# Issuing a small DRAM round trip of an attention from GpSimd instead of SyncE

## The chip, the cores and the metric

The program runs on one core of a Trainium2 chip. The metric is device time of one execution in microseconds (us); lower is better. Before the change it is 3516.77 us, the median of 3 runs (3515.63 to 3521.61). The engines are TensorE (PE, matmuls), VectorE (DVE), ScalarE (ACT), GpSimd (POOL) and SyncE (SP, which here only issues DMAs). Each engine works through its own instruction queue in order; a DMA is issued from one of these queues and then runs by itself.

## What is computed

The reference runs two blocks over a sequence of 1024 tokens of width 1024. The first block (attention and mixture of experts) is not touched. The second has two layers; each normalises the input, projects it with `w_in`, feeds three mixers (retention, a latent-query attention `mla`, and a gated linear attention), multiplies their outputs with SiLU gates and projects with `w_out`. The change is in `mla`:

```python
def block(args):                                   # one block of 128 queries, 8 heads
    qn, qp, i0 = args
    sc = (jnp.einsum('bqhd,bkhd->bhqk', qn, k_nope)
          + jnp.einsum('bqhd,bkd->bhqk', qp, k_pe)).astype(jnp.float32) * scale
    q_chunk = (i0 + jnp.arange(Q_BLOCK)) // CHUNK
    mask = key_chunk[None, :] <= q_chunk[:, None]
    sc = jnp.where(mask, sc, -jnp.inf)
    p = jax.nn.softmax(sc, axis=-1).astype(v.dtype)
    return jnp.einsum('bhqk,bkhe->bqhe', p, v)
...
mixed = jnp.concatenate([r_o * jax.nn.silu(rz), m_o * jax.nn.silu(mz),
                         g_o * jax.nn.silu(gz)], axis=-1)
x = x + gate[:, None, :] * (mixed @ w_out[l])
```

## The kernel before

`mla` (from L1580) works on four pairs of heads, each with 16 tiles (2 heads by 8 blocks of 128 queries), in one loop over 68 steps at L1723. Step n does three things: `out(n-4)`, `scores(n)` and `turn(n-2)`. `scores` computes the 128 rows of scores on PE (L1751 to L1755), their maximum on DVE (L1757) and the exponent on ACT (L1759), which also leaves each row's sum in a column of `sm`; the tile `p` serves long rows, `ps` short ones. `turn` transposes the exponents on PE (L1783) and copies them out of PSUM with ACT, either at L1785 or as a high and a low part (L80 on ACT, L81 on DVE). `out` multiplies with the values (L1795 for short rows, L1804 for long ones; copies and adds at L1797, L1806, L1807) into `u0` and `u1`. The exponents are not normalised there: the division is done once per pair, on the output.

For that, at the last tile of a pair (n % 16 == 15), `attend_sums` (L1762) takes the 128x16 sums: DVE forms reciprocals (L1765), PE transposes them (L1767), ACT copies the result to `rt`, 16x128 (L1769), a DMA stores it to DRAM (`rrd`, L1770), and two DMAs load each head's 1024 numbers back, repeated over 64 partitions (L1773), into `rb`, a tile with the tag `lo`. Nothing else passes through `rrd`. Four steps later `out` loads the gate `z` (L1707), multiplies it by `rb` on POOL (L1708) and calls `store_mix` (L1303):

```python
(eng or nc.vector).tensor_tensor(z, v, z, op=ALU.mult)
hi, lo = self.t4("tb"), self.t4("lo")
g.split(z, hi.bitcast(F32R), lo.bitcast(F32R), eng)
nc.sync.dma_start(self.mixd[0, chunk * P:chunk * P + P], hi)
nc.sync.dma_start(self.mixd[1, chunk * P:chunk * P + P], lo)
```

`eng` is POOL for the first three pairs (L1306 on POOL, then ACT writes `tb` at L80, then POOL `lo` at L81) and DVE for the fourth. The stores (L1309, L1310) go to chunk 2 + pair of `mixd`.

The same loop prefetches `w_out` in 1 MB pieces from steps 42, 52 and 58 and after the loop (`load_out`, L1816, two loads of 512 KB on SP each; the last piece into tiles `p`), and `split_out` makes parts `r` from them (ACT, POOL or DVE). When the attention is over, `layer` (L1862) loads `mixd` (`load_mix`, L1834, tiles `mx`; the first chunks are 128x5x128 floats, 320 KB, once for each of the two parts) and multiplies with `w_out` (`products`, matmuls `acc<-r,mx` at L85 to L87). Chunk 5, which the fourth pair writes, is multiplied last for the first two row blocks and is loaded separately.

The program is written as if in one order; a scheduler then sets the order on each engine from its own estimates and adds the waits. So moving a DMA to another queue can also move instructions on engines that the edit does not name.

Of the kernel before, what the change touches and what calls it, by code (L numbers as in the profile page):

```python
# [19 lines left out]
S = 1024  # L20
D = 1024
P = 128
# [1149 lines left out]
class Second:  # L1172
# [589 lines left out]
    def attend_sums(self, pair, sums, pool):  # L1762

        g, nc = self.g, self.g.nc
        nc.vector.reciprocal(sums, sums)  # L1765
        tp = self.PSs.tile([P, 512], F32, tag="S", name=g.name("rt"))
        nc.tensor.transpose(tp[0:16, 0:P], sums.rearrange("p h t -> p (h t)"), g.ident)  # L1767
        r = pool.tile([16, P], F32, tag="rt", name=g.name("rt"))
        nc.scalar.activation(r, tp[0:16, 0:P], AF.Copy)  # L1769
        nc.sync.dma_start(self.rrd[pair].rearrange("h (t c) -> (h t) c", c=P), r)  # L1770
        rb = self.t4("lo")
        for q in range(2):
            nc.sync.dma_start(rb[64 * q:64 * q + 64], self.rrd[pair, q:q + 1].broadcast_to([64, S]))  # L1773
        return rb

    def attend_turn(self, p, i, pT):
# [345 lines left out]
```

## Time and profile before

| | |
|---|---|
| runs: median (lowest to highest) | 3516.77 us (3515.63 to 3521.61) |
| profiled execution: its own time | 3515.97 us |
| its span | 3514.2 us |
| PE busy | 3299.4 us (94%) |
| ACT busy / DVE busy / POOL busy | 1825.6 / 2407.2 / 829.2 us |
| mean granted PE clock | 0.967 of full speed |
| last attention matmul of `mla`, first layer | ends at 2737.17 us of the span |
| last attention matmul of `mla`, second layer | ends at 3402.75 us of the span |

The span is the time between the first and the last instruction that the profile shows; 1.8 us of the execution's own time lie outside it. PE is the busiest engine by far, so the question for any stage is what PE waits for there. In a timeline row, the bracket at the end gives how long the engine had been idle before that instruction and what ended the idle time; a name followed by q (SPq, POOLq) is the engine's issuing queue. A DMA's row shows only its issue: when its data landed is seen from who waited for it. "L1773" is a line of the kernel; `rrd<-rt` reads "into rrd, from rt".

### The profile page before, as it was taken

The page shows a single profiled execution, that of the slowest core. Times are in us where ns is not written, and L with a number is a line of the kernel's source. Part 1 is how long each engine was busy: PE and PEld are TensorE (multiplying, and loading weights), DVE is VectorE, ACT ScalarE, POOL GpSimd, SP SyncE. Part 2 cuts the span into 40 slices and gives each one's busy share as a digit, 9 for nine tenths or more (in the row PEclk, how much of TensorE's full clock was granted, in tenths as well). Part 3 has the DMA queues.
Part 4 walks back from the last instruction along what each step waited for, and adds up shares of the span by engine and source line. Part 5 has one row for each costly group of instructions (what it writes and reads, how often), then busy time and mean ns, then how long its engine had stood idle before and what let it go on. Part 6 is the DMA issues. An engine that isn't in the chain of part 4 may idle for free. (4 is left out here: it accounts for less than half of the span.)

```text
span 3514.2 us, 44298 instructions
## 1 busy us (share of the span) xinstructions
PE 3299.4 (94%) x16904; PEld 2730.2 (78%) x16904; DVE 2407.2 (69%) x2850; ACT 1825.6 (52%) x2601; POOL 829.2 (24%) x627
## 2 busy tenths in 40 slices
PE   8999999999999969999999993999999899998988
PEld 7888878888888857888888882877777788676776
DVE  5665888799999975679999996532366443425653
ACT  3224872588878733248778772122467212244751
POOL 1121221133333231113333326321002122400120
PEclk9999999999999989999999996999999999999999
DMA  8666524699999832179999984211322632023144
GB/s 260 216 188 173 146 87 162 248 389 381 380 379 378 303 128 77 75 265 381 388 387 382 376 314 170 37 31 38 116 73 91 203 91 43 19 81 108 61 138 156
DMA packets 302967, 695.86 MB, mean 198 GB/s; under 512 B 57518, under 2 KB 154576, under 8 KB 286300
## 3 DMA queue, kind: packets, MB, share of 16 engines
q1 hardware_dynamic: 263964, 634.11, 51.8%
q0 software_dynamic: 36480, 50.45, 4.3%
q10 hardware_dynamic: 2304, 8.39, 0.6%
q8 instruction: 136, 2.23, 0.3%
q14 instruction: 83, 0.68, 0.1%
HBM read 625.59 MB, written 98.66 MB: 206 GB/s over the span
## 5 line engine op out<-in xcount | busy, mean ns | idle before, releaser
L81 DVE TENSOR_TENSOR wcut<-wraw,wcut 128x2048 fp32r<-128x2048 f32 (+1 forms) x401 | 902.7, 2267 | 66.7 <-ACT wcut L80 66.7
L80 ACT ACTIVATE wcut<-wraw 128x2048 fp32r<-128x2048 f32 (+1 forms) x401 | 754.0, 1900 | 124.8 <-PE accy L87 98.1
L85 PE MATMUL gu<-wcut,xgh 128*128 128x512 f32 x1024 | 408.7, 399 | 0.4 <-ACT xgh L80 0.4
L87 PE MATMUL gu<-wcut,xgl 128*128 128x512 f32 x1024 | 403.8, 394 | 0.0
L86 PE MATMUL gu<-wcut,xgh 128*128 128x512 f32 x1024 | 401.3, 392 | 0.0
L806 POOL DMA_INDIRECT yd<-yo,idx x64 | 171.4, 2679 | 799.8 <-DVE yo L805 780.2
L85 PE MATMUL A<-h,whi 128*128 128x512 f32 (+1 forms) x736 | 287.3, 391 | 6.2 <-ACT h L80 3.3
L87 PE MATMUL A<-h,wlo 128*128 128x512 f32 (+1 forms) x736 | 281.8, 383 | 3.8 <-DVE wlo L81 3.8
L86 PE MATMUL A<-h,whi 128*128 128x512 f32 (+1 forms) x736 | 282.8, 384 | 0.9 <-DVE h L81 0.9
L80 ACT ACTIVATE whi<-wraw 128x1024 fp32r<-128x1024 f32 (+2 forms) x86 | 70.9, 856 | 310.7 <-PE A L86 251.4
L85 PEld LDWEIGHTS gu<-wcut,xgh 128*128 128x128 f32 x1024 | 193.9, 189 | 38.4 <-ACT xgh L80 0.8
L86 PEld LDWEIGHTS gu<-wcut,xgh 128*128 128x128 f32 x1024 | 192.8, 188 | 39.3
L87 PEld LDWEIGHTS gu<-wcut,xgl 128*128 128x128 f32 x1024 | 192.4, 188 | 39.7 <-DVE xgl L81 0.9
L81 DVE TENSOR_TENSOR wlo<-wraw,whi 128x1024 fp32r<-128x1024 f32 (+2 forms) x86 | 83.1, 973 | 200.8 <-ACT whi L80 200.5
L87 PE MATMUL accy<-wcut,hl 128*128 128x512 f32 x512 | 201.9, 394 | 0.3 <-DVE hl L81 0.3
L86 PE MATMUL accy<-wcut,hh 128*128 128x512 f32 x512 | 200.6, 392 | 0.0
L85 PE MATMUL accy<-wcut,hh 128*128 128x512 f32 x512 | 199.1, 389 | 1.6 <-ACT hh L80 1.6
L746 POOL DMA_INDIRECT xg<-hd,idx x64 | 182.7, 2854 | 49.3 <-DVE idx L736 30.4
L85 PEld LDWEIGHTS A<-h,whi 128*128 128x128 f32 x736 | 144.8, 197 | 34.6 <-ACT h L80 4.5
L87 PEld LDWEIGHTS A<-h,wlo 128*128 128x128 f32 x736 | 143.8, 195 | 31.5 <-DVE wlo L81 4.7
L86 PEld LDWEIGHTS A<-h,whi 128*128 128x128 f32 x736 | 144.5, 196 | 27.6 <-issue 3.1
L1708 POOL TENSOR_TENSOR z<-z,lo 128x1024 f32<-128x1024 f32 x8 | 19.0, 2375 | 471.4 <-DMA lo<-rrd 235.8
(518 smaller groups left out, 7835.9 us busy)
## 6 DMA issues: line engine op xcount, KB each, us to landing
wraw<-in_moe_w_gate SPq DMA_DIRECT2D x128, 1024.0 KB
wraw<-in_moe_w_up SPq DMA_DIRECT2D x128, 1024.0 KB
wraw<-in_moe_w_down SPq DMA_DIRECT2D x128, 1024.0 KB
spare<-in_ada_w SPq DMA_DIRECT2D x48, 512.0 KB
wraw<-in_w_in SPq DMA_DIRECT2D x40, 512.0 KB
y<-yd SPq DMA_DIRECT2D x16, 1024.0 KB
wraw<-in_attn_w_qkv SPq DMA_DIRECT2D x12, 1024.0 KB
mx<-mixd SPq DMA_DIRECT2D x24, 512.0 KB
```

Of the source, the lines that this page charges most:

```text
L80: self.nc.scalar.activation(hi, src, AF.Copy)
L81: (lo_eng or self.nc.vector).tensor_tensor(lo, src, hi.bitcast(F32), op=ALU.subtract)
L85: mm(out, wh, xh, start=start, stop=False)
L86: mm(out, wh, xl, start=False, stop=False)
L87: mm(out, wl, xh, start=False, stop=stop)
L746: self.g.nc.gpsimd.indirect_dma_start(out=xg, out_offset=None, in_=self.hd, in_offset=bass.IndirectOffsetOnAxis(ap=idx, axis=0), bounds_ch ...
L806: st = nc.gpsimd.indirect_dma_start(out=self.yd, out_offset=bass.IndirectOffsetOnAxis(ap=yidx, axis=0), in_=y, in_offset=None, bounds_chec ...
L1708: nc.gpsimd.tensor_tensor(z, z, rb, op=ALU.mult)
```

## The change

In `attend_sums`, the store of the reciprocals and both broadcast loads are issued from POOL's queue instead of SP's. It runs for four pairs in each of two layers: 8 stores of 8 KB and 16 loads of 256 KB.

```diff
--- before.py
+++ after.py
@@ -1767,10 +1767,10 @@
         nc.tensor.transpose(tp[0:16, 0:P], sums.rearrange("p h t -> p (h t)"), g.ident)
         r = pool.tile([16, P], F32, tag="rt", name=g.name("rt"))
         nc.scalar.activation(r, tp[0:16, 0:P], AF.Copy)
-        nc.sync.dma_start(self.rrd[pair].rearrange("h (t c) -> (h t) c", c=P), r)
+        nc.gpsimd.dma_start(self.rrd[pair].rearrange("h (t c) -> (h t) c", c=P), r)
         rb = self.t4("lo")
         for q in range(2):
-            nc.sync.dma_start(rb[64 * q:64 * q + 64], self.rrd[pair, q:q + 1].broadcast_to([64, S]))
+            nc.gpsimd.dma_start(rb[64 * q:64 * q + 64], self.rrd[pair, q:q + 1].broadcast_to([64, S]))
         return rb
 
     def attend_turn(self, p, i, pT):
```

The scheduler's order moves with it. SP's queue at the end of the attention (first layer, fourth pair; `p` is the last piece of w_out, `mx` the first loads of `mixd`):

```order
 L1816 DMA p_23042<-in_w_out 128x2x512
 L1816 DMA p_23043<-in_w_out 128x2x512
-L1770 DMA rrd<-rt_22967 16x128
-L1773 DMA lo_22970<-rrd 64x1024 x2
 L1834 DMA mx_23078<-mixd 128x5x128 x2
 L1834 DMA mx_23078<-mixd 128x2x128 x2
```

The store and the two loads of the sums are gone from between the last w_out loads and the first `mx` loads.

ACT's queue in the second pair of the first layer, where the first pair's `tb` (the high part of its gated output) is made:

```order
 L80 ACTIVATE r_21236<-T_21710 128x4x128
-L80 ACTIVATE r_21236<-T_21717 128x3x128
-L1759 ACTIVATE p_21708,sm_21576<-S_21698,mx_21706 128x768
 L80 ACTIVATE tb_21667<-z_21660 128x1024
 L1806 ACTIVATE u_3820_21685<-o_21687 128x128
+L1759 ACTIVATE p_21708,sm_21576<-S_21698,mx_21706 128x768
+L80 ACTIVATE r_21236<-T_21717 128x3x128
+L1797 ACTIVATE u_3821_21686<-o_21723 64x128
 L1759 ACTIVATE ps_21733,sm_21576<-S_21726,mx_21731 128x384
 L1785 ACTIVATE r_21075<-T_21735 128x256
 L1759 ACTIVATE p_21759,sm_21576<-S_21749,mx_21757 128x640
```

`tb` and the copy behind it moved ahead of the 128x768 exponent and the 128x3x128 copy; the first two pairs of both layers read alike. In the third pair `tb` keeps its place, and there a 128x512 copy (L1785) moved ahead of the split of a w_out load.

POOL's queue in the third and fourth pairs of the first layer:

```order
 L81 TENSOR_TENSOR r_22684<-wo_22680,r_22683 128x1024
+L1770 DMA rrd<-rt_22512 16x128
+L1773 DMA lo_22515<-rrd 64x1024 x2
 L1708 TENSOR_TENSOR z_22616<-z_22616,lo_22515 128x1024
 L1306 TENSOR_TENSOR z_22616<-u_3919_22158,z_22616 128x1024
 L81 TENSOR_TENSOR lo_22624<-z_22616,tb_22623 128x1024
+L1770 DMA rrd<-rt_22967 16x128
+L1773 DMA lo_22970<-rrd 64x1024 x2
```

The three DMAs stand directly before the multiplication that needs them, behind the splits of the earlier w_out loads; the other pairs read alike, without the splits.

## Rows read from the trace of the kernel before

**Rows 1.** The page's busy time, share of the span and instructions of each engine.
```profile
PE 3299.4 (94%) x16904; PEld 2730.2 (78%) x16904; DVE 2407.2 (69%) x2850; ACT 1825.6 (52%) x2601; POOL 829.2 (24%) x627
```

**Rows 2.** PE's waits, 2540 to 3514: us in total, times, longest us.
```profile
PE acc L85 <- DMA mx<-mixd: 16.5, 4, 5.4
...
PE S L1751 <- ACT ps L1759: 10.1, 8, 2.9
```

**Rows 3.** SP's timeline, first layer: start us, us, engine line op out<-in, count.
```profile
2609.08 0.30 SPq L1770 DMA_DIRECT2D rrd<-rt  x1
2610.44 1.12 SPq L1773 DMA_DIRECT2D lo<-rrd  x2
...
2696.29 0.42 SPq L1770 DMA_DIRECT2D rrd<-rt  x1
2700.06 1.09 SPq L1773 DMA_DIRECT2D lo<-rrd  x2
...
2729.43 3.71 SPq L1816 DMA_DIRECT2D p<-in_w_out  x2
2733.45 0.33 SPq L1770 DMA_DIRECT2D rrd<-rt  x1
2736.64 1.34 SPq L1773 DMA_DIRECT2D lo<-rrd  x2
2738.08 3.89 SPq L1834 DMA_DIRECT2D mx<-mixd  x6
```

**Rows 4.** PE's timeline, matmuls after long idles: [idle before <-releaser].
```profile
2699.61 0.39 PE L1751 MATMUL S<-h,qs 96*128 96x256 f32 x1 [2.85 <-ACT ps L1759]
...
2742.53 0.80 PE L85 MATMUL acc<-r,mx 128*128 128x512 f32 x1 [5.36 <-DMA mx<-mixd]
...
3328.79 0.50 PE L1751 MATMUL S<-h,r 96*128 96x512 f32 x1 [1.64 <-ACT ps L1759]
...
3364.10 0.39 PE L1751 MATMUL S<-h,qs 96*128 96x256 f32 x1 [1.94 <-ACT ps L1759]
```

**Rows 5.** The chain of waits, second layer, first pair: start us, us, what.
```profile
3272.58 2.89 DMA rrd<-rt
...
3276.02 3.87 DMA lo<-rrd
```

**Rows 6.** ACT's timeline at tb, both layers, and the instructions ahead of one.
```profile
2620.47 1.06 ACT L80 ACTIVATE tb<-z 128x1024 fp32r<-128x1024 f32 x1
...
2661.51 1.06 ACT L80 ACTIVATE tb<-z 128x1024 fp32r<-128x1024 f32 x1 [0.42 <-POOL z L1306]
...
3282.59 0.48 ACT L80 ACTIVATE r<-T 128x384 fp32r<-128x384 f32 x1
3282.96 0.91 ACT L1759 ACTIVATE p<-S,mx 128x768 f32<-128x768 f32 x1
...
3326.95 1.06 ACT L80 ACTIVATE tb<-z 128x1024 fp32r<-128x1024 f32 x1 [1.26 <-POOL z L1306]
...
3375.32 1.06 ACT L80 ACTIVATE tb<-z 128x1024 fp32r<-128x1024 f32 x1 [1.54 <-POOL z L1306]
```

**Rows 7.** POOL's timeline, first layer, first pair: the second multiplication.
```profile
2617.55 2.39 POOL L1306 TENSOR_TENSOR z<-u,z 128x1024 f32<-128x1024 f32 x1
```

**Rows 8.** DMA issues of SP (L1770) and POOL: count, ns min/median/max; last row landing.
```profile
L1770 SPq DMA_DIRECT2D rrd<-rt x8: 302/316/416, 2609.1 to 3399.0; - x8
...
L1136 POOL DMA_DIRECT2D md<-adab x12: 484/513/526, 91.7 to 288.4; - x12
...
L250 POOL DMA_DIRECT2D kd<-fh x16: 580/586/730, 70.1 to 284.1; - x16
...
DMA to landing us min/median/max: 3.2/4.0/7.6
```

**Rows 9.** Busy time by stretch, then granted PE clock, DMA share, GB/s.
```profile
core 0: us, PE busy (x) PEld busy (x) DVE busy (x) ACT busy (x) POOL busy (x), PEclk, DMA share, GB/s
2732.00:2737.00 5.00, 4.06 (x31) 3.31 (x28) 2.65 (x7) 3.83 (x11) 0.00 (x0) 1.00 0.44 139
...
2742.50:2748.00 5.50, 5.47 (x12) 4.01 (x13) 2.45 (x2) 1.06 (x1) 1.43 (x1) 0.50 0.83 233
3328.80:3334.00 5.20, 5.20 (x34) 4.25 (x35) 2.89 (x5) 4.11 (x12) 1.65 (x1) 1.00 0.77 280
3366.00:3369.20 3.20, 3.20 (x14) 2.82 (x13) 1.34 (x3) 3.00 (x8) 0.00 (x0) 0.50 0.58 166
```

## The prediction

> **What bounds the kernel now.** I read the page first: TensorE (PE) is busy for 94% of the span [rows 1], so time is won or lost only where PE idles or runs at the lower clock. The list of PE's waits over the two attention stages comes next [rows 2]: 16.5 us on loads of `mx`, in few long waits, and 10.1 us in eight waits of a score matmul on ScalarE's (ACT) exponent. Neither names the moved DMAs, so I followed both back.
>
> The first kind sits at the end of each layer's attention. SP issues its queue in order [rows 3]: the last weight load `p<-in_w_out` ends its issue at 2733.14, the store of the sums goes at 2733.45, the loads of the sums wait for its landing until 2736.64, and only then, at 2738.08, come the `mx` loads. PE's first product starts at 2742.53 after 5.36 us idle [rows 4]. The `mx` loads need nothing that the sums make: they only stand behind them.
>
> The second kind sits behind ACT's `tb<-z`. In the second layer's first pair the store lands 2.89 us after issue and the loads 3.87 after theirs [rows 5]; then GpSimd (POOL) does two multiplications, and ACT, which reaches `tb` earlier, waits. In the second pair ACT waits 1.26 us at `tb` [rows 6], and PE 1.64 at the score behind it [rows 4]: PE's loss is ACT's plus 0.4. In the first layer's first pair the store lands after 1.36 (2609.08 to 2610.44) [rows 3], POOL ends at 2619.94 [rows 7], `tb` starts at 2620.47 without a wait, and in the second pair it waits 0.42 [rows 6].
>
> **The change part by part.** Eight stores and sixteen loads leave SP for POOL; no byte is added.
>
> *Issue.* SP spends 0.316 us on a store, POOL 0.513 on its smallest plain DMA [rows 8]. POOL is not busy between the sums and the multiplication that needs them, and nothing that could run sooner is queued behind its wait, so only the landing counts.
>
> *D, how much later the sums arrive from POOL.* No row has this store or load on POOL. Nearest: POOL's 128 KB loads land in 3.2, 4.0 and 7.6 us (least, median, most) [rows 8]; SP's 256 KB load in 3.87 [rows 5]. Bringing 4.0 to 256 KB at 233 GB/s [rows 9] adds 0.56, so the load comes about 0.7 later; the store adds at least its 0.2 of issue. I take D = 0.9. From below: a store landing everywhere in the 1.36 of the first layer gives -1.5 in the second. From above: the 7.6 [rows 8] gives +3.6.
>
> The Trainium skill, page "DMA: Bandwidth & Descriptors", section "Latency and other measured facts", speaks against the change: it gives about 1 us to the first byte for a DMA from GpSimd and about 0.6 for one from SP. By it, two DMAs in a chain would make D 0.8 by estimate, and the sum below 0.4 us lower; no run here has shown that for these transfers.
>
> *ACT's order.* In pairs one and two of each layer `tb` now stands ahead of a 128x384 copy and a 128x768 exponent, 0.48 and 0.91 us [rows 6]. With the sums arriving as before, ACT waits 1.4 us longer, and what PE needs next (that exponent) is behind `tb`. In the first layer's first pair 0.5 of it is slack (2619.94 to 2620.47). Loss: 0.9 + 3 x 1.4 = 5.1 us, plus 4 x D = 3.6.
>
> *Clock.* After 1.94 us of PE idle (3364.10) [rows 4] the granted clock fell to 0.50 for 3.2 us, that is 1.2 of 2.4 GHz, and 1.6 us were lost; after 1.64 (3328.79) it stayed at 1.00 [rows 9]. The four idles would be 2.2 (0.9 + 0.9 + 0.4), 3.1, 3.8 and 3.9 us, all above 1.94: 4 x 1.6 = 6.4. Bounds: none to all four. Loss of the first two pairs together: 15.1 us.
>
> *Third pair.* The store went at 2696.29 behind w_out loads and landed 3.77 later [rows 3]. POOL's own queue has none of those in front; I take the sums 1 us earlier there, net of D. In the second layer `tb` waited 1.54 [rows 6], so 1.0 comes back, and in the first I count nothing. PE idled 2.85 and 1.94 there [rows 4], while ACT waited for w_out; four transposes now stand ahead of the waiting score, and ACT does a copy before its split, worth 0.45 to 1.0, taken as 0.6 each. The 1.94 falls below 1.64, and its clock dip goes: 1.6. Gain 0.6 + 0.6 + 1.0 + 1.6 = 3.8; bounds 0 and 6.
>
> *End of attention.* SP goes from `p` straight to `mx`: 2733.2 instead of 2738.08, 4.8 us earlier. The path to PE is 4.45 (2738.08 to 2742.53), but `p`'s 1 MB, issued just before, is still arriving. Full gain is 4.8; if 1 MB of `p`, 0.5 MB of sums and 640 KB of `mx` (2.2 MB) pass one after another at 233 GB/s from the middle of `p`'s issue (2731.3), that is 9.6 us, the product starts at 2740.9 and the gain is 1.6. At 2732 to 2737 the DMA engines are busy 0.44 [rows 9], so much room is left: I take 3.5. Idle becomes 1.9, and the half-clock stretch of 5.5 us behind it [rows 9] shrinks to the 3.2 of the third pair, 1.15 us back. Two layers: 2 x 4.65 = 9.3; bounds 3 and 13. The fourth pair's sums may come later by D at no cost: their product chunk is multiplied last.
>
> *Sum.* 15.1 - 3.8 - 9.3 = +2.0 us on the profiled execution's 3515.97, which is 0.8 below the median of the runs: **3518.0 us**.
>
> **The rivals.**
>
> *Faster: POOL's sums come no later.* What takes 2.9 us in the second layer, against 1.4 in the first, is not explained by the rows; from another queue it may be 1.4 in both. Then D is 0 in the first layer and -1.5 in the second: 5.1 - 3.0, one dip of 1.6, so 3.7 lost, against 13.1 won: -9.4, 3506.6 us. Against it: every POOL row has longer issue and no landing under 3.2.
>
> *Slower: the two landings take the place of SP's queue.* If each of POOL's two steps costs some 0.8 to 1.5 more, D is 2.5. Five waits on the sums reach PE (four above and the second layer's third pair): 5 x 1.6 = 8 more than my sum, 3526 us. It decides from D of about 2.1. For it: POOL's 7.6 us landings [rows 8]. Against it: their median of 4.0.
>
> *Slower at the end: `mx` gains nothing beyond its place in the queue.* With `p`, the sums and `mx` sharing the DMA engines, PE starts 1.6 us sooner per layer and the clock stretch stays: 3.2 won instead of 9.3, 3524.1 us. Against it: the 0.44 above.
> The Trainium skill says so in "Issuing engines are not separate DMA queues" of the same page: DMAs from several engines share the same 16 DMA engines, and only issue time is saved. The SP rows [rows 3] show a wait for a landing, not issue, and whether that rule reaches it no run has shown yet.
>
> *The change does not do what it says*: no; the order of SP's and POOL's queues has it.
>
> **How the numbers follow.** About 0.2% (7 us) is what a measurement of this kernel can tell from no change: same is 3509.7 to 3523.8. My sum with its bounds (D from 0.3 to 1.8, dips two to four) covers 3511 to 3523: chance 0.41. Faster, by the first rival or by a larger gain at the end, 0.33. Slower, by D 0.18 and by the end 0.08, 0.26. The range 3505 to 3528 takes in the first two rivals at their priced values and leaves out their far tails.
>
> **What would show it.** Right: `mx` issued right behind `p`, PE's waits on `mx` down from 16.5 to about 9.5 us, waits behind `tb` in the first two pairs up by some 9, with half clock behind them, and POOL's landings some 0.9 later in all. Wrong: `tb` waits as long as before, or the sums arrive earlier from POOL; or PE starts its products less than 2 us sooner after the last attention matmul.

## The result, and the profile after

The change makes the kernel slower: 3542.69 us, the median of 5 runs (3536.91 to 3547.84), against 3516.77 us before. The ratio is 1.0073 (95% interval 1.0062 to 1.0084), 25.9 us more, and lies outside the predicted range. The profiled execution of the changed kernel took 3543.91 us, with a span of 3541.9 us and a mean granted clock of 0.962; its span is 27.7 us longer than that of the kernel before.

The page's line of busy time, of the changed kernel:

```profile
PE 3313.9 (94%) x16904; PEld 2742.5 (77%) x16904; DVE 2409.5 (68%) x2850; ACT 1825.8 (52%) x2601; POOL 843.5 (24%) x651
```

Against [rows 1], PE does the same 16904 matmuls, but is busy 14.5 us longer, at a mean granted clock of 0.962 instead of 0.967: so about half of the loss goes with the lower clock, and the rest is idle time. PE's waits over the two attention stages of the changed kernel (us in total, times, longest):

```profile
PE acc L85 <- DMA mx<-mixd: 20.3, 5, 7.4
PE o L1795 <- DVE u L1807: 16.6, 10, 3.1
...
PE S L1751 <- ACT ps L1759: 2.7, 4, 1.5
```

The wait on `mx` was to fall from 16.5 us [rows 2] to about 9.5 and rose to 20.3. The wait of a score on `ps` fell from 10.1 us to 2.7; in its place a multiplication with the values waits on `u` (L1807) for 16.6 us, 3.2 before. But for the third pair's 2.85 and 1.94 us [rows 4], both are mainly the wait behind `tb`: since `tb` moved ahead on ACT, another matmul stands behind it. Where it lies is seen in PE's timeline of the changed kernel (start, us, ..., idle before and what ended it):

```profile
2625.04 0.79 PE L1795 MATMUL o<-r,vf 128*128 128x128 f32 x2 [2.70 <-DVE u L1807]
...
2670.14 0.49 PE L1795 MATMUL o<-r,vf 128*128 128x128 f32 x2 [2.22 <-DVE u L1807]
...
2744.68 0.50 PE L85 MATMUL acc<-r,mx 128*128 128x512 f32 x1 [1.07 <-DMA mx<-mixd]
...
2762.41 0.79 PE L85 MATMUL acc<-r,mx 128*128 128x512 f32 x1 [7.43 <-DMA mx<-mixd]
...
2782.11 0.77 PE L85 MATMUL acc<-r,mx 128*128 128x512 f32 x1 [3.04 <-DMA mx<-mixd]
...
3302.43 0.49 PE L1795 MATMUL o<-r,vf 128*128 128x128 f32 x2 [3.14 <-DVE u L1807]
...
3347.02 0.49 PE L1795 MATMUL o<-r,vf 128*128 128x128 f32 x2 [2.79 <-DVE u L1807]
...
3397.19 0.80 PE L1795 MATMUL o<-r,vf 128*128 128x128 f32 x2 [3.11 <-DVE u L1807]
...
3426.01 0.50 PE L85 MATMUL acc<-r,mx 128*128 128x512 f32 x1 [1.43 <-DMA mx<-mixd]
...
3442.47 0.80 PE L85 MATMUL acc<-r,mx 128*128 128x512 f32 x1 [7.28 <-DMA mx<-mixd]
```

The first product after the attention comes after 1.07 and 1.43 us instead of 5.36 [rows 4], as intended. But 36 products later, at 2762.41 and 3442.47, PE waits more than 7 us for `mx` again; the kernel before had no wait there. SP's timeline of the changed kernel says why:

```profile
2735.82 3.78 SPq L1816 DMA_DIRECT2D p<-in_w_out  x2
2739.69 4.34 SPq L1834 DMA_DIRECT2D mx<-mixd  x6
2757.74 0.33 SPq L1309 DMA_DIRECT2D mixd<-tb  x1
2759.00 0.33 SPq L1310 DMA_DIRECT2D mixd<-lo  x1
2759.39 3.40 SPq L1834 DMA_DIRECT2D mx<-mixd  x6
```

The first six `mx` loads go right behind `p`. Then SP stands at L1309, the store of the fourth pair's output, until ACT has made `tb`: 13.6 us by SP's list of waits, 4.2 before. Behind that store, in the same queue, stand the next six `mx` loads, and chunks 6 and 7 of the second row block, which the 37th product needs, are the first of them. The kernel before has the same queue from here on:

```profile
2746.30 0.33 SPq L1309 DMA_DIRECT2D mixd<-tb  x1
2747.56 0.33 SPq L1310 DMA_DIRECT2D mixd<-lo  x1
2747.95 3.48 SPq L1834 DMA_DIRECT2D mx<-mixd  x6
```

Everything ahead of the layer's end lies 6.4 us later in the changed kernel (ACT's `rt` of the fourth pair starts at 2733.17 before and 2739.61 after). L1309 went from 2746.30 to 2757.74, 11.4 us: so the fourth pair's output comes 5.0 us later in its own right. That is the sums' doing, as POOL's timeline of the changed kernel shows for the third and fourth pair of the first layer:

```profile
2702.82 0.56 POOL L1770 DMA_DIRECT2D rrd<-rt  x1
2706.93 1.03 POOL L1773 DMA_DIRECT2D lo<-rrd  x2 [3.56 <-issue]
2711.42 2.38 POOL L1708 TENSOR_TENSOR z<-z,lo 128x1024 f32<-128x1024 f32 x1 [3.46 <-DMA lo<-rrd]
...
2740.15 0.56 POOL L1770 DMA_DIRECT2D rrd<-rt  x1 [20.38 <-ACT r L80]
2746.00 1.03 POOL L1773 DMA_DIRECT2D lo<-rrd  x2 [5.29 <-issue]
2752.99 2.38 POOL L1708 TENSOR_TENSOR z<-z,lo 128x1024 f32<-128x1024 f32 x1 [5.96 <-DMA lo<-rrd]
```

In the fourth pair the store's landing took 5.85 us (2740.15 to 2746.00) and the loads 6.99 more (to 2752.99), 12.84 together; before, the store went at 2733.45 [rows 3] and the multiplication began at 2741.58, 8.13 later. The DMA engines while the sums were under way, in windows of the kernel before (two rows) and of the changed kernel (two rows); the DMA engines' busy share is the number before the last, GB/s the last:

```profile
2733.40:2736.60 3.20, 2.51 (x20) 2.15 (x20) 1.70 (x4) 2.24 (x7) 0.00 (x0) 1.00 0.56 172
2736.60:2741.60 5.00, 0.57 (x6) 0.38 (x4) 4.71 (x5) 1.10 (x2) 0.02 (x1) 0.98 0.69 186
...
2739.00:2746.00 7.00, 4.61 (x29) 3.36 (x28) 4.97 (x9) 4.28 (x10) 0.56 (x1) 1.00 0.84 230
2746.00:2753.00 7.00, 6.13 (x27) 4.72 (x27) 1.84 (x2) 0.00 (x0) 1.04 (x3) 1.00 0.64 152
```

While the store landed, the share was 0.84 instead of 0.56, and by SP's queue the bytes were those of `p` and `mx`. While the loads landed it was 0.64, no higher than the 0.69 before: for the loads the mean share doesn't show the crowding, and that reading rests on the experiments.

The granted clock after four of these waits, from the windows of the changed kernel (PEclk is the third number from the end):

```profile
2625.00:2630.00 5.00, 4.96 (x19) 4.46 (x20) 1.29 (x2) 3.00 (x10) 1.87 (x1) 0.50 0.73 252
...
2670.10:2675.00 4.90, 4.86 (x31) 3.98 (x32) 2.60 (x6) 4.21 (x13) 1.87 (x1) 1.00 0.72 255
...
2762.40:2768.00 5.60, 5.59 (x13) 4.04 (x14) 0.00 (x0) 0.00 (x0) 0.00 (x0) 0.50 0.93 277
...
3302.40:3306.00 3.60, 3.57 (x16) 2.89 (x17) 1.29 (x2) 2.84 (x9) 1.87 (x1) 0.72 0.61 244
```

After idles of 2.70, 7.43 and 3.14 us the clock was 1.2 of 2.4 GHz for all or part of the stretch; after 2.22 us it stayed at 2.4 GHz.

**Where the 27.7 us are.** ACT's copy to `rt` (L1769) runs once a pair and is a milestone in both traces. The shift grows by 11.2 us from the first pair's `rt` to the third's, the two layers together (4.9 and 0.5, then 3.2 and 2.6); by 0.1 from the third's to the fourth's (-0.7 and 0.9); and by 14.6 from the fourth's to the next layer's first `rt`, or to the end of the span (8.8 and 5.9). The remaining 1.8 are there already at the first pair, ahead of anything that was changed.

Not all of the 14.6 lies at the layers' ends. If the nth matmul of one trace is set against the nth of the other, the shift grows by 6.2 and 4.4 from the fourth `rt` to 2800 and to 3502 of the kernel before, 10.6 in all. Another 1.4 come behind the last product, and 2.6 far behind the first layer's end, 2.4 of them in the second layer's projections before its attention. There PE's long idles are the same (1.42, 3.58 and 3.43 us in both traces), but the clock differs, as the windows of the kernel before (first row) and of the changed kernel show:

```profile
3198.90:3219.30 20.40, 12.92 (x47) 9.57 (x47) 15.10 (x18) 9.71 (x12) 0.00 (x0) 0.92 0.54 183
...
3211.80:3234.50 22.70, 15.69 (x47) 11.88 (x46) 15.13 (x18) 9.65 (x12) 0.00 (x0) 0.73 0.51 167
```

Nothing that was changed stands there. From 2800 to 3240 of the kernel before, where no edit reaches, the shift of the other traces below changes by -1.7 to +2.5 us, and here by +2.5; so these 4.0 us are not counted as a loss of the layers' ends.

### The profile page after: what moved, and what is told of

It is laid out like the page before. It is cut to its first block, busy times and chain, and to the rows that moved or that the text cites. A ratio compares the mean times of both kernels' runs of the same rounds, so it can differ in the third digit from the quotient of the medians.

```text
span 3541.9 us, 44296 instructions
## 1 busy us (share of the span) xinstructions
PE 3313.9 (94%) x16904; PEld 2742.5 (77%) x16904; DVE 2409.5 (68%) x2850; ACT 1825.8 (52%) x2601; POOL 843.5 (24%) x651
## 3 DMA queue, kind: packets, MB, share of 16 engines
q8 instruction: 136, 2.23, 0.3%
## 5 line engine op out<-in xcount | busy, mean ns | idle before, releaser
L86 PEld LDWEIGHTS A<-h,whi 128*128 128x128 f32 x736 | 144.6, 197 | 27.7 <-issue 3.1
L85 PE MATMUL acc<-r,mx 128*128 128x512 f32 x256 | 105.0, 410 | 23.0 <-DMA mx<-mixd 20.3
```

Source lines behind the costliest of these rows:

```text
L85: mm(out, wh, xh, start=start, stop=False)
L86: mm(out, wh, xl, start=False, stop=False)
```

## The experiments

After the result the theory was: two separate losses. *At the layer's end*, the `mx` loads now pass the fourth pair's sums and crowd their two landings, and the second stop in SP's queue, L1309, hands that delay to PE. *In pairs one to three*, the earlier `tb` and somewhat later sums make PE wait, with half clock behind it. The rivals: POOL's DMAs are simply slow (then every POOL store and load is late, with or without company), or the new order alone does it. "Pair 4" is the fourth pair of heads, `pair == 3` in the code. Each ratio is against the kernel before, run again beside it (medians 3518.73, 3519.75 and 3520.2 us).

### Only the fourth pair from GpSimd

```diff
-        nc.sync.dma_start(self.rrd[pair]..., r)
+        (nc.gpsimd if pair == 3 else nc.sync).dma_start(self.rrd[pair]..., r)
-            nc.sync.dma_start(rb[64 * q:64 * q + 64], ...)
+            (nc.gpsimd if pair == 3 else nc.sync).dma_start(rb[64 * q:64 * q + 64], ...)
```

> Only the fourth pair's store and loads of the sums go to POOL; pairs one to three stay on SP. No instruction of PE, ACT or DVE moves. My theory is that the loss at the end of the attention has nothing to do with the first three pairs: the sums of the fourth pair take 12 to 13 us from store to multiplication (8 before), SP stands at the store of that pair's output, and loads of mx that need nothing from it stand behind. Then PE waits some 7 us in the products after 36 matmuls, the first product still starts about 4 us sooner than before, and the time is that of before plus 12 to 17 us, some 3531 us. Rival: the first pairs' later sums pushed the end out of step; then with them back on SP the end gains its 4 us per layer without the 7 us wait, and the time is 3505 to 3512 us.

Measured: 3532.14 us, ratio 1.0035 (1.0022 to 1.0048). ACT, PE and DVE keep the order of the kernel before, and still the pattern of the changed kernel's layer end is there: the first product waits 1.97 us, and 36 products later, in PE's timeline of this kernel:

```profile
2760.10 0.80 PE L85 MATMUL acc<-r,mx 128*128 128x512 f32 x1 [7.50 <-DMA mx<-mixd]
```

The store's landing took 6.7 us, the loads 7.4. So the layer's end alone carries half of the loss, as the theory had it, without any change of order on ACT or PE.

### Only the first three pairs from GpSimd

```diff
+        (nc.sync if pair == 3 else nc.gpsimd).dma_start(self.rrd[pair]..., r)
...
+            (nc.sync if pair == 3 else nc.gpsimd).dma_start(rb[64 * q:64 * q + 64], ...)
```

> The first three pairs' sums go to POOL, the fourth's stay on SP: PE, ACT and DVE have the order of the changed kernel up to the third pair, the end is as before. If the parts add, the time is that of before plus 10 to 12 us, about 3528 us, with PE waits of 2.5 to 3.2 us behind tb in the first two pairs of both layers, and the first product starting about 5.3 us after the last attention matmul, as before. Rival: the loss of the whole change is at the end alone, and this one is within 3 us of before.

Measured: 3533.99 us, ratio 1.0042 (1.0030 to 1.0054), somewhat above what was expected. ACT has the changed kernel's order; ACT waits 2.23, 2.32, 2.74 and 2.79 us at `tb` in the first two pairs, where before it waited not at all, 0.42, 1.12 and 1.26 [rows 6]. The third pair costs more here than in the changed kernel: PE idles 3.75 and 4.00 us behind its `tb`, where it was 0.81 and 3.11, and the first product waits 6.36 and 6.37 us, not the 5.3 expected. The two halves add: 0.35% and 0.42% make 0.77%, against 0.73% for the whole.

### Only the loads of the first three pairs

```diff
-            nc.sync.dma_start(rb[64 * q:64 * q + 64], ...)
+            (nc.sync if pair == 3 else nc.gpsimd).dma_start(rb[64 * q:64 * q + 64], ...)
```

> Of the first three pairs only the loads of the sums go to POOL, the store stays on SP. PE, ACT and DVE keep the order of before, so this is the price of POOL's landing alone. Theory, order: the loss of pairs one and two in the changed kernel is ACT's new order (tb ahead of the exponent), and the landing is only some 0.3 us later; then this kernel is within 3 us of before (3514 to 3520 us) and PE's idles behind tb grow by under 0.5 us each. Rival, landing: POOL's loads arrive 1 us or more later each time; then PE's four idles grow by 1 us each, clock dips come behind them, and the time is 3524 us or more.

Measured: 3525.09 us, ratio 1.0013 (1.0004 to 1.0022). Here ACT, PE and DVE keep the order of before, so this is the price of the later sums alone. From `rt` to POOL's multiplication it took 7.40, 7.57, 9.02 and 8.68 us in the first two pairs of each layer; before, 6.29, 7.19, 7.90 and 8.05. ACT waits 0.49, 0.77, 1.92 and 1.88 us at `tb`, and in the second layer the clock dips: 0.91 in 3280 to 3300 and in 3320 to 3340, 1.00 before in both. The sums are 0.8 us later in the mean, 0.66 of it ahead of the issue of the loads (2.32, 2.15, 4.12 and 3.83 us after `rt`, 1.65, 1.69, 3.20 and 3.24 before). From issue to multiplication POOL's loads took 5.08, 5.42, 4.90 and 4.85 us, SP's before 4.64, 5.50, 4.70 and 4.81: without company a load from POOL is hardly slower. The time itself lies in the rival's range, but the distance to the kernel before, some 4.6 us by the ratio, lies between the two theories (3 and 7), so only the size is told: later sums alone cost 0.13%, about a third of the first three pairs' 0.42%. The third pair's sums, 1.3 and 0.9 us later here, are part of it.

### Only the store of the first three pairs

```diff
-        nc.sync.dma_start(self.rrd[pair]..., r)
+        (nc.sync if pair == 3 else nc.gpsimd).dma_start(self.rrd[pair]..., r)
```

> Of the first three pairs only the store of the sums goes to POOL; SP issues the loads as before. The store from POOL lands as soon as from SP (3.1 us in the fourth pair's run), so the sums come no later than before by more than 0.5 us; but the scheduler moves tb on ACT even further forward than in the changed kernel, ahead of the 128x4x128 copy too (2.0 us of ACT work instead of 1.4). Theory, order: ACT waits 3 us or more at tb in the first two pairs, PE idles 3 to 4 us behind it with half clock after, and the time is 12 to 20 us above before, at least as much as with all three DMAs on POOL (12 to 17). Rival, landing: the loss of the first pairs comes from the loads issued by POOL; here it is gone, and the time is within 5 us of before.

Measured: 3529.61 us, ratio 1.0024 (1.0014 to 1.0034), below what the theory gave and above the rival. This kernel has the new order without POOL's loads, and its sums come no later (6.39, 7.26, 7.65 and 6.23 us from `rt` to the multiplication); `tb` moved still further ahead than in the changed kernel, and ACT waits 3.59, 4.42, 4.82 and 3.42 us at it. PE's idles behind it were 1.93, 2.71, 3.16 and 1.71 us, and the clock was lower after three of them. The columns are those of the windows above:

```profile
2623.90:2628.00 4.10, 4.07 (x17) 3.58 (x18) 1.89 (x3) 3.40 (x10) 1.85 (x1) 0.58 0.68 255
...
3338.60:3343.00 4.40, 4.24 (x28) 3.44 (x28) 2.18 (x4) 4.10 (x13) 1.89 (x1) 1.00 0.67 246
```

So the order, here with the store from POOL, is the larger part (0.24%) and the later sums of the run before the smaller (0.13%); together 0.37%, near the 0.42% of the first three pairs. It is no exact division, since this order isn't that of the changed kernel.

### The fourth pair's sums and its output stores from GpSimd

```diff
-        nc.sync.dma_start(self.mixd[0, chunk * P:chunk * P + P], hi)
-        nc.sync.dma_start(self.mixd[1, chunk * P:chunk * P + P], lo)
+        (q or nc.sync).dma_start(self.mixd[0, chunk * P:chunk * P + P], hi)
+        (q or nc.sync).dma_start(self.mixd[1, chunk * P:chunk * P + P], lo)
...
+                self.store_mix(on, z, 2 + pair, nc.gpsimd if pair < 3 else None, nc.gpsimd if pair == 3 else None)
```

The sums of pair 4 go from GpSimd as in the first experiment. With L1309 gone from SP's queue, nothing there should hold the `mx` loads.

> The fourth pair's sums go to POOL, and so do the two stores of its gated output, so that SP goes from the last w_out loads through all mx loads that do not need them. Theory, SP's queue: the 7.3 us wait of PE after 36 product matmuls is that of loads standing behind those stores; it goes, the first product keeps its 4 us, and the time is 3503 to 3508 us, 9 to 14 less than before. Rival, late data: PE needs the fourth pair's chunk itself (or the mx loads do not fit into the DMA engines' time), the wait only moves to a later matmul, and the time is 3512 us or more.

Measured: 3524.25 us, ratio 1.0016 (1.0008 to 1.0025): better than the first experiment, but still slower than before, and not the gain expected: the rival held. The wait after 36 products is gone, which shows that L1309 caused it. SP stops at the next thing that needs the same data, the load of chunk 5; SP's list of waits of this kernel:

```profile
SPq L1834 <- DMA mixd<-tb: 15.0, 1, 15.0
```

PE's timeline of this kernel:

```profile
2772.05 0.80 PE L85 MATMUL acc<-r,mx 128*128 128x512 f32 x1 [11.64 <-DVE hn L1846]
```

Behind that load stand `x` and the next row block's `mx`, and PE pays 11.64 us later on. The sums were as late as before the edit: 6.75 us for the store, 7.5 for the loads.

### The same, and the chunk-5 loads from GpSimd too

```diff
-                nc.sync.dma_start(m[:, j, a0:a1].bitcast(F32), ...)
+                (nc.gpsimd if a0 == 5 else nc.sync).dma_start(m[:, j, a0:a1].bitcast(F32), ...)
```

> As the run with the fourth pair's sums and output stores on POOL, and the loads of its chunk of mx for the first two row blocks on POOL too, so that no instruction of SP waits for anything that the fourth pair's sums make. Theory, SP's queue: in that run SP stood 15 us at those loads, and the third row block's loads stood behind; PE's 11.6 us wait there falls to the 2.75 of before, the first product keeps its 4 us, and the time is 3507 to 3513 us. Rival, late data: the chunk itself comes late, PE waits 3 us or more at its first matmuls with a clock dip behind, and the time is 3516 us or more.

Measured: 3523.71 us, ratio 1.0012 (1.0003 to 1.0021), no better: the rival in that expectation held. The stop moved one step further again, to the load of `x`. SP's list of waits of this kernel:

```profile
SPq L1894 <- DMA mixd<-tb: 15.9, 1, 15.9
```

`x` needs a buffer that comes free only behind the output. PE waits 4.07 us on `mx` at 2768.60 and 6.03 on `hn` at 2778.77. Taking away a wait of SP's three times running (before the `mx` loads, at L1309, at chunk 5) moved it and never removed it in the first layer. This points to the fourth pair's sums as what bounds that layer's end, and they were late (6.6 us for the store, 9.0 for the loads); no run that only brings them sooner shows it alone. With the nth matmul set against the nth, as above, the first layer's end loses 8.0, 7.2 and 8.6 us in the first experiment, the last one and this one, and the second's 5.8, -1.5 and 0.6: by these traces, one for each kernel, clearing SP's queue took the loss from the second layer only. Why the first kept it is not shown.

### The fourth pair's store alone, and its loads alone

```diff
+        (nc.gpsimd if pair == 3 else nc.sync).dma_start(self.rrd[pair]..., r)
```

> Of the fourth pair only the store of the sums goes to POOL; SP still issues the two loads and, behind their wait, mx. So nothing but the 1 MB of w_out is ahead of POOL's store. Theory, crowding: the 5.9 us that the store needed in the changed kernel are mx loads that were issued around it, not POOL; here it lands in 3 to 4 us as it did from SP, the first product waits some 5.4 us after the last attention matmul, and the time is within 3 us of before. Rival, POOL is slow: the store takes 5 us or more here too, the mx loads go out 2 us later than before, and the time is 4 to 8 us above before.

Measured: 3519.97 us, ratio 1.0001 (0.9992 to 1.0010), no difference. The loads, still SP's, wait for the landing ahead of `mx`, so the store has only `p` for company. POOL's timeline of this kernel:

```profile
2735.90 0.66 POOL L1770 DMA_DIRECT2D rrd<-rt  x1 [20.48 <-ACT r L80]
```

SP's timeline of this kernel:

```profile
2739.04 1.09 SPq L1773 DMA_DIRECT2D lo<-rrd  x2
2740.23 4.29 SPq L1834 DMA_DIRECT2D mx<-mixd  x6
```

The landing took 3.14 us from POOL against 3.19 from SP [rows 3]: a store from POOL isn't slow, and that rival is out for the store; for the loads, those of the first three pairs speak against it (4.85 to 5.42 us). The other half of the pair:

```diff
+            (nc.gpsimd if pair == 3 else nc.sync).dma_start(rb[64 * q:64 * q + 64], ...)
```

> Of the fourth pair only the two loads of the sums go to POOL; SP issues the store, and mx right behind it without a wait. Theory, crowding: the store, ahead of mx in SP's queue, lands in 3 to 4 us; the loads, issued when mx is on its way, need 6 to 7.5 us instead of 4.9 to the multiplication; the first product starts 4 us sooner, PE waits 4 to 6 us after 36 matmuls, and the time is 4 to 10 us above before. Rival, the loads are not crowded: they need under 5.3 us, the wait after 36 matmuls is under 3 us, and the time is within 2 us of before or under it.

Measured: 3528.61 us, ratio 1.0030 (1.0018 to 1.0042), near the upper edge of the theory's 4 to 10 us. The store stands ahead of `mx` on SP and lands in 4.5 us, but `mx` follows it without waiting, and POOL's loads come into the middle of it: 9.0 us (2735.93 to 2744.95) where it took 4.9. PE then waits 7.21 us at the 37th product, as in the changed kernel. Which queue issues makes no difference to the store; what was let past the sums does.

### A dose of it: the first row block's loads only

```diff
-                nc.sync.dma_start(m[:, j, a0:a1].bitcast(F32), ...)
+                (nc.gpsimd if t == 0 and a0 == 0 else nc.sync).dma_start(m[:, j, a0:a1].bitcast(F32), ...)
```

The sums stay on SP, and only 640 KB of `mx` (two loads of 320 KB) go ahead of them, from POOL.

> The sums stay on SP in all pairs, as before; instead the first two loads of mx (chunks 0 to 4 of the first row block, 640 KB, which need nothing of the attention's last pair) go to POOL, where nothing of the sums stands in front; all other mx loads stay behind the sums on SP, and the order of the rest is that of before but for the second row block's chunks 6 and 7, which go ahead of the output stores. Theory: what the sums lost in the changed kernel was their place ahead of 1.7 MB of mx; with only 640 KB let past, and early, the sums' way takes 8 to 9 us as before, PE starts its products within 1.5 us after the last attention matmul instead of 5.3, waits some 2 us more for chunks 6 and 7, and the time is 5 to 12 us under before, 3506 to 3513 us. Rival: the end is bound by the sums' chain (store, loads, two multiplications, stores, loads of the last chunk, and what SP issues behind), not by PE's start; then the idle time moves to later matmuls and the time is within 3 us of before.

Measured: 3518.00 us, ratio 0.9994 (0.9985 to 1.0004), no difference that can be told; the rival held. SP's timeline of this kernel:

```profile
2737.51 0.33 SPq L1770 DMA_DIRECT2D rrd<-rt  x1
2742.67 1.09 SPq L1773 DMA_DIRECT2D lo<-rrd  x2
```

The store now needs 5.16 us from SP's own queue, 2 more than before, for 640 KB of company. The first product starts after 3.42 us idle instead of 5.36, and 5.79 us of waiting for `hn` come at 2774.12. What the products win at the front is lost again behind it, with the sums later, and the time stays as it was.

### No round trip at all

```diff
-        nc.scalar.activation(r, tp[0:16, 0:P], AF.Copy)
-        nc.sync.dma_start(self.rrd[pair]..., r)
+        nc.vector.tensor_copy(out=bc..., in_=sums...broadcast_to([P, NT, 2, 64]))
+        for j0 in (0, 4):
...
+                nc.tensor.transpose(tp[:, j - j0], bc[:, j * P:j * P + P], g.ident)
+            nc.scalar.activation(rb[:, j0 * P:j0 * P + 4 * P], tp.rearrange("p a c -> p (a c)"), AF.Copy)
```

DVE repeats the reciprocals in SBUF, PE transposes them (8 matmuls a pair) and ACT copies them out; no DMA is left in it.

> No DRAM round trip of the sums in any pair: DVE repeats the reciprocals over 64 columns per head into the free tile tb, PE transposes them in eight 128x128 pieces and ACT copies them to the same tile as the loads filled. Eight times one DVE copy (1.2 us), eight transposes (0.9 us) and two ACT copies of 512 (0.6 us each) are added, a transpose and a copy fall away. Theory: what the sums' way through DRAM costs in all three places (tb in the first pairs, the third pair, mx behind it on SP) goes: some 5 us behind tb with two clock dips of 1.6, 4.2 us of idle and 2.7 of half clock at each layer's end, against 6 to 7 us of PE work added: 3503 to 3510 us. Rival: the sums' wait was cover for other work, ACT and the order that the scheduler makes of it become the bound, and the time is 3515 us or more.

Measured: 3540.47 us, ratio 1.0061 (1.0048 to 1.0074), a miss. The scheduler made another order of it. SP's timeline of this kernel:

```profile
2730.63 8.26 SPq L1815 DMA_DIRECT2D p<-in_w_out  x2
2746.05 0.34 SPq L1309 DMA_DIRECT2D mixd<-tb  x1
2746.50 0.37 SPq L1833 DMA_DIRECT2D mx<-mixd  x1
2748.37 0.33 SPq L1310 DMA_DIRECT2D mixd<-lo  x1
2748.76 7.25 SPq L1833 DMA_DIRECT2D mx<-mixd  x11
```

All `mx` loads stand behind the first output store, L1309, and the first product waits 7.36 us. So it does not tell what the round trip costs: it is inconclusive on that. No run beat the kernel before. A third `mx` buffer, or a second `u0`, which might loosen the layer's end, was not measured.

## Why the prediction was wrong

**The step that failed** is the last sentence of *End of attention*: "The fourth pair's sums may come later by D at no cost: their product chunk is multiplied last." It looked at what the sums feed in PE's order and not at what waits for them in SP's. The trace of the kernel before had it: the store of the output, L1309, stands in SP's queue ahead of half of the `mx` loads (2746.30, then six at 2747.95). And "later by D" was the wrong size for this pair. SP's stop for the landing [rows 3] had two effects, and only one was counted. It held `mx` back, 4.8 us; it also kept 1.57 MB of `mx` (four loads of 320 KB, two of 128) back until 8 KB of sums had landed and the loads of 512 KB were issued. Without it the two landings went from 8.13 to 12.84 us in the first layer and from 8.0 to 11.9 in the second.

Term by term:

- *End of attention*, predicted -9.3. The front gain came, as sized: measured from the fourth pair's `rt`, the first product is 4.3 and 3.9 us earlier (predicted 3.5 each), and the first products run at full clock. It was given back and more: the shift over the two ends is +10.6, so 18.8 us were lost behind the first products (10.5 and 8.3). In the first layer: L1309 is 5.0 us late in its own right; the third row block's first product, 2770.14 before and 2782.11 after, is 5.5 late; the half-clock stretch that stood at the front now stands behind the long wait, on the bound path; after the third block's 3.04 us the clock is 0.65 in 2785 to 2790, where the kernel before dipped too (0.71 in 2770 to 2775, behind 2.75 us). The first experiment shows this part alone: 0.35%, some 12 us.
- *First two pairs*, predicted +15.1, measured +11.2: right in mechanism, too large in size. PE's idles behind `tb` were 2.70, 2.22, 3.14 and 2.79 us, 10.9 in all, where 13.0 were forecast (2.2, 3.1, 3.8, 3.9) and 4.2 stood before (0.30, 0.80, 1.49 and 1.64); the clock after three of them lost some 6.6 us (from the windows, us times one minus the clock), where four dips were to cost 6.4: near the forecast by luck, with one dip fewer and each dearer. *D* was 1.7, 0.3, 0.5 and 0.0 us in the four pairs (`rt` to the multiplication: 7.97, 7.48, 8.44 and 8.08 after), a mean of 0.6 against 0.9 forecast. The run with POOL's loads alone, and the one with the store alone, show both terms, the later sums the smaller and the order the larger, as forecast (3.6 and 5.1, and the clock).
- *Third pair*, predicted -3.8, measured +0.1. The gains in front came: the score that waited 2.85 and 1.94 us [rows 4] waited 1.50 and 0.73, and the sums reached POOL's multiplication 0.6 and 0.7 us sooner after `rt` (1.0 forecast), though the store's landing took 4.11 and 4.72 us even from POOL's own queue. But the forecast let `tb`'s wait shrink by that 1.0; ACT, no longer held in front, came to `tb` sooner by more than the sums did, and waited 1.46 and 3.72 us instead of 0.17 and 1.54. PE's idle behind it went from 0.90 to 3.11 us in the second layer, with a clock of 0.50 in 3397.2 to 3402. A wait that was removed ahead of a fixed arrival came back at the arrival.
- *Sum*: the first two pairs 3.9 better than forecast, the third 3.9 worse, the ends 19.9 worse, 4.0 in stretches that the change doesn't reach, and 1.8 ahead of it: 2.0 - 3.9 + 3.9 + 19.9 + 4.0 + 1.8 = 27.7. The forecast of 3518.0 us adds the 2.0 to the profiled execution; on the median of the runs it would be 3518.8.

**The rivals.** "Slower at the end: `mx` gains nothing beyond its place in the queue" named the right place and resource, but it priced a smaller gain (3524.1 us), not a loss: it asked what the shared DMA engines do to `mx`, and not what `mx` does to the sums. The rival with D 2.5 had the right sign for the wrong pairs; nowhere but in the fourth was D above 1.7. By the Trainium skill, "DMA: Bandwidth & Descriptors", section "Issuing engines are not separate DMA queues", another issuing engine saves only issue time, and the transfers interleave on the same 16 engines. The trace agrees: a landing depended on the bytes under way, and the same store took 3.1 us from POOL and 5.2 from SP. The first-byte figures of the Trainium skill's same page, section "Latency and other measured facts", about 1 us from GpSimd and 0.6 from SP, made D 0.8 by estimate; measured it is 0.6 in the mean, with 0.0 to 1.7 single, and for the fourth pair's store nothing (3.14 and 3.19).

## What to carry to other kernels

A small DMA that waits at the head of an in-order queue also keeps what is queued behind it out of the DMA engines; before moving it to a free queue, ask what will be let past it and whether its data is the bound. If it is, follow every later stop on the same data in the old queue: removing the first stop only sends the engine to the next. And with a scheduler between code and queue, read the new order of the engines that the edit does not name, as a moved DMA may put another engine's instruction ahead of the data it waits for.

## What the runs showed of the hardware that was not expected

- A small store's landing by its company, all at the end of the first layer's attention, behind 1 MB of `p`: with no `mx`, 3.2 us from SP and 3.1 from POOL; with 640 KB of `mx` ahead, 5.2; with six or more `mx` loads in the same moments, 5.85, 6.6, 6.7 and 6.75 from POOL in four kernels, and 4.5 from SP with the store ahead of them in its queue. The 512 KB of sums that followed took 4.9 to 5.1 us in the first two cases, and 7.0 to 9.0 beside the six or more.
- PE's clock after an idle is not told by the idle's length alone: after 1.93 us it was 0.58 over the next 4.1 us, after 2.22 us in another kernel it stayed at 1.00.
- Not explained: in pairs one and two the store lands in 1.4 us in the first layer and 2.9 in the second [rows 3, 5], with SP; in one run's second layer, the dose's second pair, it landed in 1.4 too (3319.45 to 3320.85).
